# A hybrid attention block in fp32: linear attention's small products set in groups among dense projection products, pooling's vector work ahead of them, output projection by token halves

## The chip, the cores and the metric

The kernel runs on one core of a Trainium2 chip. The metric is the device time of one execution in microseconds, the median of a few runs. TensorE (PE) multiplies matrices; its weight loads (PEld) run beside its products. VectorE (DVE), ScalarE (ACT) and GpSimd (POOL) do the elementwise work, and SyncE's queue (SP) issues nearly all transfers between the DRAM and the on-chip memory. Products land in eight banks of the accumulation memory (PSUM) and are read from there by DVE or ACT.

## The reference

One layer over 1024 tokens of width 1024, batch 1:

```
h = rmsnorm(x, ln1);  z = h @ w_in            # columns split among three mixers
y_pool: trailing means over 2, 4, 8, 16 tokens, minus the input, a 64x64 product per group, a scale
y_gla : linear attention, 4 heads of 64, chunks of 64 tokens:
        q_in = q*exp(b-ref), k_in = k*exp(ref-b), att = tril(q_in k_in^T), o_intra = att v
        kv_n = (k*exp(b_last-b))^T v ;  S_n+1 = dec_n*S_n + kv_n ;  o_inter = (q*exp(b)) S_n
        per-head rmsnorm of o_intra + o_inter, times silu(g)
y_fox : softmax attention with forgetting, 8 heads of 64, causal
x = x + [y_pool, y_gla, y_fox] @ w_o
h = rmsnorm(x, ln2);  x = x + (silu(h@w_gate) * (h@w_up)) @ w_down ;  out = rmsnorm(x, ln_f)
```

## The kernel before, in words

**Tiling.** All data are fp32. A dense product is made of three products of rounded parts: an operand `a` is held as a high part `ah` (rounded, by ACT) and a low part `al = a - ah` (by DVE or POOL), and `gemm` (L133) adds `ah*bh + ah*bl + al*bh` into one PSUM bank, in a fixed order in each bank. A projection of 128 columns of `w_in` (`project`, L243) loads its 128x1024 weights, splits them (`load_w`, `split_w`), and makes two banks (token halves `c` of 512) of 8 x 3 = 24 products each, 48 in all. The small products of linear attention (transposes, `pkv`, `pat`, `po`) and pooling's `py` are plain fp32 and are not split.

**Stages.** (1) The first norm and `gv` (`psg`). (2) `decays` (L262): log gates and their running sums `bc`, on ACT and DVE. (3) `pool_in`: projections `zp0`, `zp1` into `u0`, `u1`. (4) `gla_qk(j)` (L285) for the two head pairs `j`: differences of `bc` on POOL (`d1`, `d2`), their exponentials on ACT, the projections `zgk`, `zgq`, their products with the exponentials, and eight transposes `pk` (L312) into `k2t`. (5) `pool_tile` (L396), tile 1 then tile 0: a chain of shifted sums on DVE (L399, L400, L411, L413 to L415), two products `py` (L420), a scaling on ACT (L421) and a transfer to the DRAM (L422). (6) `gla_state` (L316): 30 products `pkv` of 64x64 per pair and a 15-step scan on DVE (L330). (7) `fox_values(0)` (L426): `psv`, 8 token blocks of 24 products of 256 columns. (8) `gla_out(j)` (L339): the projection `zgg` with silu, and for both halves `c`: 8 products `pat` (L353), a masked copy (L355), for each of 8 (block, head) pairs one product with `attb` (L364) and then two 64x64 products with the state (L368) into `po`, the norm, four transposes `pot` (L384). (9) `fox_qk` and `fox_attend` for four head pairs `p`, each projection among the attention of the pair before. (10) The output projection `pxa` (first four 128-row blocks of the mixed activations) and `pxb` (the last four), 24 products per 128-token block `tb`, 8 blocks each; after each `pxb` block the second norm `norm2` with its transposes into `raw`. (11) The feed-forward products by a seven-product scheme: left operands `left(i)` (L660), weights `right(fi)`, products `m` (L710) and `d` (L916). Products 3 and 5 read only the first token half.

**What sets the order.** The program is traced in the order of the code and a scheduler then orders each engine's instructions by a simulated timeline: program order is the priority, and what is not ready in that simulation, by its inputs or by its buffer, is passed over. On the chip each engine runs its list in order. Buffers are slots of 128x1024 fp32. Rings hand them out strictly in program order: `p` (6 slots, most vector tiles), `pp` (3), `wr` (2, raw weights) and `w` (4, the high and low parts of two weight tiles). A tile may be written only when the tile that had its slot before is read for the last time, by transfers too. PSUM has `s` (3 banks), `pt` (2), `o` (1) and `gm` (2, all dense projections).

Ring `p` before, from the decays on: la0, la1, lft, ones, Fc, d2_0, gk0, gq0, d2_1, gk1, gq1, ps2_1, ps4_1, ps8_1, ps16_1, pd1, py1, ps2_0, ps4_0, pd0, py0, sg0, gy0, ... (each on the slot of the tile six places ahead of it). Ring `w`: zp0, zp1, zgk0, zgq0, zgk1, zgq1, the two halves of wfv0, zgg0, zgg1, zq0, zk0, ... (each on the slots of the one two places ahead). In the output projection `mr4` and `mix4`, the first buffers that `pxb` needs, have the slots of `wo3h` and `wo3l`, which the last `pxa` product reads.

Of the kernel before, what the change touches and what calls it, by code (L numbers as in the profile page):

```python
# [18 lines left out]
P = 128  # L19
# [12 lines left out]
def tile_hybrid_block(ctx: ExitStack, tc, x, w_fv, w_gv, w_zt, w_o, w_gu, w_down, ln, w_pool, w_a3, chans, b_f, consts, out):  # L32
# [107 lines left out]


# [101 lines left out]
    def project(ct, name):  # L243
        hi, lo = load_w(w_zt[:, ct, :], name, eng=POOL)
        for c in range(2):
            ps = PS("gm", f"{name}p{c}")
            gemm(ps, [((hi[:, k * P:(k + 1) * P], lo[:, k * P:(k + 1) * P]), chunk(hT, k, c)) for k in range(NK)])
            yield slice(c * 512, c * 512 + 512), ps
# [11 lines left out]
    decs, bcs = [], []  # L260
# [24 lines left out]
    def gla_qk(j):  # L285
        bc = bcs[j]
        b3 = e3(bc)
        dc = cst.tile([P, 16], F32, name=f"dec{j}")
        decs.append(dc)
        ACT.activation(dc, b3[:, :, 63], AF.Exp, scale=1.0 / 16)  # L290
        d1, d2, eq = G(f"d1_{j}"), R(f"d2_{j}"), G(f"eq{j}")
        POOL.tensor_tensor(out=e3(d1), in0=b3, in1=b3[:, :, 31:32].broadcast_to([P, 16, 64]), op=ALU.subtract)
        POOL.tensor_tensor(out=e3(d2), in0=b3[:, :, 63:64].broadcast_to([P, 16, 64]), in1=b3, op=ALU.subtract)
        ACT.activation(eq, d1, AF.Exp, scale=1.0 / 16)
        ACT.activation(d1, d1, AF.Exp, scale=-1.0 / 16)
        ACT.activation(d2, d2, AF.Exp, scale=1.0 / 16)
        ACT.activation(bc, bc, AF.Exp, scale=1.0 / 16)
        k_, q_ = R(f"gk{j}"), R(f"gq{j}")
        for csl, ps in project(8 + 2 * j, f"zgk{j}"):
            ACT.activation(k_[:, csl], ps, AF.Copy)  # L300
        DVE.tensor_tensor(out=d2, in0=k_, in1=d2, op=ALU.mult)
        DVE.tensor_tensor(out=d1, in0=k_, in1=d1, op=ALU.mult)
        for csl, ps in project(9 + 2 * j, f"zgq{j}"):
            ACT.activation(q_[:, csl], ps, AF.Copy, scale=0.125)
        DVE.tensor_tensor(out=eq, in0=q_, in1=eq, op=ALU.mult)
        POOL.tensor_tensor(out=bc, in0=q_, in1=bc, op=ALU.mult)
        kt = G(f"k2t{j}")
        for h in range(2):
            pt = PS("pt", f"pk{j}_{h}")
            for i in range(4):  # L310
                tb = 4 * h + i
                PE.transpose(pt[:, i * P:(i + 1) * P], d2[:, tb * P:(tb + 1) * P], ident)  # L312
            ACT.activation(kt[:, h * 512:(h + 1) * 512], pt, AF.Copy)
        return eq, d1, bc, kt

    def gla_state(j, kt):  # L316

        St = G(f"St{j}")
        POOL.memset(St[:, 0:64], 0.0)
        ps = [PS("s", f"pkv{j}_{q}") for q in range(2)]  # L320
        for n in range(15):
            tb, r = n // 2, slice(64 * (n % 2), 64 * (n % 2) + 64)
            o = ps[n % 2][:, (n // 2) * 64:(n // 2) * 64 + 64]
            for a in range(2):
                PE.matmul(o[64 * a:64 * a + 64], kt[r, tb * P + 64 * a:tb * P + 64 * a + 64],
                          gv[tb // 4][r, (tb % 4) * 256 + (2 * j + a) * 64:(tb % 4) * 256 + (2 * j + a + 1) * 64],
                          start=True, stop=True)
        for n in range(15):
            o = ps[n % 2][:, (n // 2) * 64:(n // 2) * 64 + 64]
            DVE.scalar_tensor_tensor(out=St[:, (n + 1) * 64:(n + 2) * 64], in0=St[:, n * 64:(n + 1) * 64],  # L330
                                     scalar=decs[j][:, n:n + 1], in1=o, op0=ALU.mult, op1=ALU.add)
        free(f"k2t{j}")
        return St

# [4 lines left out]
    def gla_out(j, qi, ki, qe, St):  # L339
        sg = R(f"sg{j}")  # L340
        for csl, ps in project(12 + j, f"zgg{j}"):
            ACT.activation(sg[:, csl], ps, AF.Silu)
        y = R(f"gy{j}")
        for c in range(2):
            pat = [PS("pt", f"pat{j}_{c}_{a}") for a in range(2)]
            po = [PS("s", f"po{j}_{c}_{a}") for a in range(2)]
            ab = attb[c]
            for i in range(4):
                tb = 4 * c + i
                tsl = slice(tb * P, (tb + 1) * P)  # L350
                for a in range(2):
                    r = slice(64 * a, 64 * a + 64)
                    PE.matmul(pat[a][:, i * P:(i + 1) * P], ki[r, tsl], qi[r, tsl], start=True, stop=True)  # L353
            for a in range(2):
                DVE.copy_predicated(ab[:, a * 512:(a + 1) * 512].rearrange("p (m t) -> p m t", t=P),  # L355
                                    gmask.rearrange("p (o t) -> p o t", o=1).broadcast_to([P, 4, P]),
                                    pat[a].rearrange("p (m t) -> p m t", t=P))
            for i in range(4):
                tb = 4 * c + i
                for a in range(2):  # L360
                    r = slice(64 * a, 64 * a + 64)
# [647 lines left out]
```

## Time and profile before

| | |
|---|---|
| median of 3 runs (lowest to highest) | 1199.56 us (1198.48 to 1200.44) |
| the profiled execution | 1203.56 us |
| its span, first to last instruction | 1201.8 us |
| mean granted TensorE clock | 0.979 of full speed |
| PE busy in the span | 97% |
| DVE / ACT / POOL busy | 67% / 44% / 33% |

The profile is one execution. The span is what the views cover; the profiled execution is 1.8 us longer than its span and 4.0 us (0.33%) above the median of the runs. A matmul's recorded duration is its pipelined time; what a stream of them costs is read from the distance of their starts.

### The profile page before, as it was taken

To read this page: it belongs to the slowest core of one execution; us is meant where nothing else is said; L and a number is where in the kernel's file an instruction comes from. 1 tells how busy PE (TensorE), PEld (TensorE's weight loads), DVE (VectorE), ACT (ScalarE), POOL (GpSimd) and SP (SyncE) were. 2 spreads that over 40 slices of the span, in tenths; PEclk is the share of its full clock that TensorE was granted. 3 is DMA by queue.
4 is the path that set the end of the run, shared out by engine and by line. 5 is a ranking of instruction groups with operands and counts; after the bars stand their busy time and mean duration, and the time that the engine had idled before them with its cause. 6 is when DMAs were issued, how large, how long until landed. Compare 5 with 4: busy or idle time off the path is not lost.

```text
span 1201.8 us, 15933 instructions
## 1 busy us (share of the span) xinstructions
PE 1159.9 (97%) x5928; PEld 974.8 (81%) x5928; DVE 810.2 (67%) x1328; ACT 530.9 (44%) x965; POOL 390.9 (33%) x285
## 2 busy tenths in 40 slices
PE   6999999999999989899999999999999999999995
PEld 6878788889988778777888888888888888888874
DVE  7567612278748676468998768676776685766674
ACT  6362121257656745346444334443343344334353
POOL 2163122243333823331022220122202270660873
PEclk9999889899999999899999999999999999999998
DMA  6121111111122522221153331323224588333223
GB/s 244 35 71 53 54 35 53 36 55 47 47 62 77 169 91 97 79 105 53 53 155 112 111 120 65 131 93 118 95 90 148 214 322 288 109 96 118 63 97 140
DMA packets 53565, 126.34 MB, mean 105 GB/s; under 512 B 4792, under 2 KB 10344, under 8 KB 53488
## 3 DMA queue, kind: packets, MB, share of 16 engines
q1 hardware_dynamic: 53056, 123.75, 30.7%
q0 software_dynamic: 432, 1.57, 0.4%
q8 instruction: 46, 0.75, 0.3%
q14 instruction: 31, 0.25, 0.1%
HBM read 93.03 MB, written 32.28 MB: 104 GB/s over the span
## 4 chain that ended last, share of the span: by engine, by line
PE 84%; DVE 5%; DMA 3%; issue 3%; POOL 3%; ACT 2%; POOLq 0%; SPq 0%; ACTq 0%; DVEq 0%
PE m L710 35%; PE d L916 16%; PE pxa L138 4%; PE psv L138 3%; PE o L524 3%; PE pt L510 2%; PE s L484 1%; PE zq0p L138 1%; PE zgg0p L138 1%; PE s L485 1%; DMA mr<-mixd 1%; PE psg L138 1%; PE po L364 1%; PE zq3p L138 1%; PE zgg1p L138 1%
## 5 line engine op out<-in xcount | busy, mean ns | idle before, releaser
L710 PE MATMUL m<-hA_0h,wr 128*128 128x512 f32 x616 | 214.3, 390 | 0.6 <-ACT hr L641 0.5
L710 PE MATMUL m<-hA_1h,wr 128*128 128x512 f32 x616 | 214.6, 389 | 0.0
L710 PEld LDWEIGHTS m<-hA_0h,wr 128*128 128x128 f32 x616 | 115.6, 188 | 24.9 <-ACT hr L641 1.1
L710 PEld LDWEIGHTS m<-hA_1h,wr 128*128 128x128 f32 x616 | 115.7, 188 | 23.9
L916 PE MATMUL d<-hw,ha 128*128 128x512 f32 x308 | 120.0, 392 | 5.3 <-ACT hw L815 5.3
L710 PE MATMUL m<-hA_0l,wr 128*128 128x512 f32 x308 | 119.9, 389 | 1.7 <-DVE hA_0l L671 1.7
L916 PE MATMUL d<-lw,ha 128*128 128x512 f32 x308 | 120.4, 391 | 0.8 <-DVE lw L816 0.8
L710 PE MATMUL m<-hA_1l,wr 128*128 128x512 f32 x308 | 119.8, 389 | 0.0
L762 POOL TENSOR_TENSOR cg<-cu,cu 128x512 f32<-128x512 f32 x11 | 19.2, 1742 | 308.7 <-DVE cu L739 308.7
L916 PE MATMUL d<-hw,la 128*128 128x512 f32 x308 | 118.8, 391 | 0.0
L694 ACT ACTIVATE wr<-ws 128x512 fp32r<-128x512 f32 x110 | 69.5, 631 | 109.2 <-DVE ws L693 54.9
L695 DVE TENSOR_TENSOR wr<-ws,wr 128x512 fp32r<-128x512 f32 x110 | 75.9, 696 | 26.0 <-ACT wr L694 26.0
L816 DVE TENSOR_TENSOR la<-ra,ha 128x1024 fp32r<-128x1024 f32 (+1 forms) x42 | 58.2, 1392 | 29.0 <-ACT ha L815 21.5
L808 POOL TENSOR_TENSOR rw<-wd,wd 128x512 f32<-128x512 f32 x33 | 56.4, 1737 | 51.3 <-PE d L916 46.6
L916 PEld LDWEIGHTS d<-hw,ha 128*128 128x128 f32 x308 | 58.1, 189 | 17.8 <-ACT hw L815 5.7
L710 PEld LDWEIGHTS m<-hA_0l,wr 128*128 128x128 f32 x308 | 57.8, 188 | 14.2 <-DVE hA_0l L671 2.2
L916 PEld LDWEIGHTS d<-lw,ha 128*128 128x128 f32 x308 | 58.3, 189 | 13.3 <-DVE lw L816 1.2
L815 ACT ACTIVATE ha<-ra 128x1024 fp32r<-128x1024 f32 (+1 forms) x42 | 41.2, 987 | 61.6 <-DMA ra<-cd 56.0
L916 PEld LDWEIGHTS d<-hw,la 128*128 128x128 f32 x308 | 58.1, 189 | 12.1
L710 PEld LDWEIGHTS m<-hA_1l,wr 128*128 128x128 f32 x308 | 57.8, 188 | 12.1
L499 POOL TENSOR_TENSOR pb<-pb,rl 128x128 f32<-128x128 f32 (+3 forms) x32 | 38.1, 1196 | 83.4 <-DVE rl L496 66.5
L816 DVE TENSOR_TENSOR lw<-rw,hw 128x1024 fp32r<-128x1024 f32 (+1 forms) x30 | 45.7, 1535 | 27.3 <-ACT hw L815 27.2
(391 smaller groups left out, 2764.1 us busy)
## 6 DMA issues: line engine op xcount, KB each, us to landing
ra<-cd SPq DMA_DIRECT2D x35, 512.0 KB, 3.7
wu<-in_w_gu_dram SPq DMA_DIRECT2D x22, 512.0 KB, 4.3
wg<-in_w_gu_dram SPq DMA_DIRECT2D x22, 512.0 KB, 3.7
wd<-in_w_down_dram SPq DMA_DIRECT2D x22, 512.0 KB, 6.5
cd<-cg SPq DMA_DIRECT2D x11, 512.0 KB, 4.6
cd<-cs SPq DMA_DIRECT2D x11, 512.0 KB, 6.2
cd<-cu SPq DMA_DIRECT2D x11, 512.0 KB, 7.5
fb<-Fd SPq DMA_DIRECT2D x8, 512.0 KB, 4.5
```

What stands on the lines that cost most here:

```text
L138: PE.matmul(ps, a, b, start=(n == 0), stop=(n == last))
L499: POOL.tensor_tensor(out=pb[:, 0:W], in0=pb[:, 0:W], in1=rl[:, 0:1].broadcast_to([P, W]), op=ALU.mult)
L510: PE.transpose(pt[:, o0:o0 + P], Pb[i][:, (2 * n + b) * P:(2 * n + b + 1) * P], ident)
L524: PE.matmul(*args, start=(kb == 0 and n_ == 0), stop=(last and n_ == 1))
L694: ACT.activation(hi, src, AF.Copy)
L695: e2.tensor_tensor(out=lo, in0=src, in1=f(hi), op=ALU.subtract)
L710: PE.matmul(ps, a, b, start=(n == 0), stop=(n == 11))
L762: POOL.tensor_tensor(out=t_[:, 0:512], in0=a11, in1=a12, op=ALU.add)
L808: POOL.tensor_tensor(out=raw_[:, j * 512:j * 512 + 512], in0=wd[h0, j0 + j][:, e0, :], in1=wd[h1, j0 + j][:, e1, :], op=op)
L815: ACT.activation(hi[:, sl], src, AF.Copy)
L816: DVE.tensor_tensor(out=lo[:, sl], in0=src, in1=f(hi[:, sl]), op=ALU.subtract)
L916: PE.matmul(banks[t], a[:, o], b[:, ns], start=(j0 + j == 0 and m == 0), stop=(j0 + j == NF // 2 - 1 and m == 2))
```

## The change

The small products become lists of functions that a projection calls between its dense products (`woven`, `smalls`). `Gla` takes the place of `gla_qk`, `gla_state` and `gla_out`. Within a part of `outputs`, four products with `attb` come first and then eight with the state. `pool_tile` is traced ahead of all of linear attention. The weights of the six projections of linear attention are split on DVE and no longer on POOL. The last head pair's attention runs m = 1, 0, 3, 2 in place of 3, 1, 2, 0; the output projection's halves `g` are tokens 0 to 511 and 512 to 1023; products 3 and 5 of the feed-forward get their left operands, and `start(0)` its weights, after four of the eight `pxb` blocks.

Ring `p` after: la0, la1, lft, ones, Fc, ps2_1, ps4_1, ps8_1, ps16_1, pd1, py1, ps2_0, ps4_0, pd0, py0, d2_0, gk0, gq0, sg0, gy0, d2_1, gk1, gq1, sg1, gy1, ... Ring `w` after: zp0, zp1, zgk0, zgq0, zgg0, zgk1, zgq1, zgg1, the two halves of wfv0, zq0, zk0, ...

```
+    def woven(ps, terms, smalls=()):
+        done = 0
+        for i, ((ah, al), (bh, bl)) in enumerate(terms):
+            for n, (a, b) in enumerate(((ah, bh), (ah, bl), (al, bh))):
+                PE.matmul(ps, a, b, start=(i == 0 and n == 0), stop=(i == len(terms) - 1 and n == 2))
+            while done < len(smalls) and (done + 1) * len(terms) <= (i + 1) * len(smalls):
+                smalls[done]()
+                done += 1
...
-    def project(ct, name):
-        hi, lo = load_w(w_zt[:, ct, :], name, eng=POOL)
+    def project(ct, name, smalls=((), ()), eng=None):
+        hi, lo = load_w(w_zt[:, ct, :], name, eng=eng or POOL)
         for c in range(2):
             ps = PS("gm", f"{name}p{c}")
-            gemm(ps, [...])
+            woven(ps, [...], smalls[c])
...
+    class Gla:
+        def keys(self, smalls=((), ())):
+            j, k_ = self.j, R(f"gk{self.j}")
+            for csl, ps in project(8 + 2 * j, f"zgk{j}", smalls, eng=DVE):
+                ACT.activation(k_[:, csl], ps, AF.Copy)
+            DVE.tensor_tensor(out=self.d2, in0=k_, in1=self.d2, op=ALU.mult)
+            DVE.tensor_tensor(out=self.d1, in0=k_, in1=self.d1, op=ALU.mult)
...
+        def outputs(self, c):
+            def part(i2):
...
+                both = [(i, a) for i in (2 * i2, 2 * i2 + 1) for a in range(2)]
+                for i, a in both:
+                    h = 2 * j + a
+                    PE.matmul(po[a][:, i * 64:i * 64 + 64], attb[c][:, (4 * a + i) * P:(4 * a + i + 1) * P],
+                              gv[c][:, i * 256 + h * 64:i * 256 + (h + 1) * 64], start=(i == 0), stop=False)
+                for i, a in both:
+                    r = slice(64 * a, 64 * a + 64)
+                    for q in range(2):
+                        n = 2 * (4 * c + i) + q
+                        PE.matmul(po[a][64 * q:64 * q + 64, i * 64:i * 64 + 64], self.bc[r, n * 64:(n + 1) * 64],
+                                  self.St[r, n * 64:(n + 1) * 64], start=False, stop=(i == 3))
+                if i2:
+                    normed()
...
     us = [pool_in(j) for j in range(2)]
-    g0 = gla_qk(0)
-    g1 = gla_qk(1)
     pool_tile(1, us[1])
     pool_tile(0, us[0])
     free("misc")
-    st0 = gla_state(0, g0[3])
-    st1 = gla_state(1, g1[3])
-    V = fox_values(0)
-    gla_out(0, g0[0], g0[1], g0[2], st0)
-    gla_out(1, g1[0], g1[1], g1[2], st1)
+    A = Gla(0)
+    A.keys()
+    A.queries(((), A.turn_keys()))
+    A.gates((A.state(), A.within(0)))
+    B = Gla(1)
+    B.keys((A.within(1) + A.outputs(0), A.outputs(1) + A.turned(0)))
+    B.queries((A.turned(1), B.turn_keys()))
+    B.gates((B.state(), B.within(0)))
+    o_ = [B.outputs(0), B.outputs(1)]
+    V = fox_values(0, (B.within(1), o_[0][:1], o_[0][1:], o_[1][:1], o_[1][1:] + B.turned(0), B.turned(1), (), ()))
     ops = fox_qk(0)
...
-        for a, m in ([...] if p < 3 else [(a, m) for m in (3, 1, 2, 0) for a in range(2)]):
+        for a, m in ([...] if p < 3 else [(a, m) for m in (1, 0, 3, 2) for a in range(2)]):
...
-            SP.dma_start(src, mixd[k].rearrange("p (c g t) -> p c g t", c=2, g=2)[:, :, g])
+            SP.dma_start(src, mixd[k, :, g * 512:(g + 1) * 512])
...
-        for tb in (2 * g, 2 * g + 1, 2 * g + 4, 2 * g + 5):
+        for tb in range(4 * g, 4 * g + 4):
...
-    mixes = [load_mix(4, g) for g in (1, 0)][::-1]
-    for tb in (2, 3, 6, 7, 0, 1, 4, 5):
-        g = (tb // 2) % 2
-        out_proj(tb, xs[tb], mixes[g], ws, "pxb")
...
-    first = [start(fi) for fi in range(2)]
+    mixes = [load_mix(4, 0), None]
+    first = []
+    for tb in range(NT):
+        if tb == 2:
+            mixes[1] = load_mix(4, 1)
+        if tb == 4:
+            free(*[f"mix{k}_0" for k in range(4, 8)])
+            for i in (3, 5):
+                left(i, *lefts[i])
+            first.append(start(0))
+        out_proj(tb, xs[tb], mixes[tb // 4], ws, "pxb")
+        SP.dma_start(x3d[tb], xs[tb])
+        norm2(tb, xs[tb])
+        free(f"xa{tb}")
...
+    first.append(start(1))
     for i in (3, 5, 4, 1, 2, 7, 6):
-        left(i, *lefts[i])
+        if i not in (3, 5):
+            left(i, *lefts[i])
```

## Rows read from the trace of the kernel before

**Rows 1.** The page's first two parts: PE's busy time, its share of the span and its instructions; the TensorE clock granted in 40 slices of the span, in tenths (9 is 90% or more).

```profile
PE 1159.9 (97%) x5928; PEld 974.8 (81%) x5928; DVE 810.2 (67%) x1328; ACT 530.9 (44%) x965; POOL 390.9 (33%) x285
...
PEclk9999889899999999899999999999999999999998
```

**Rows 2.** Busy time by stretch. Columns: the stretch in us and its length, then busy us (and instructions) of PE, PEld, DVE, ACT, POOL, the mean granted clock (1.00 is 2.4 GHz, 0.50 is 1.2 GHz), the share of the DMA engines' time, GB/s.

```profile
128.00:136.00 8.00, 7.65 (x22) 4.52 (x22) 3.96 (x11) 1.82 (x4) 0.00 (x0) 0.57 0.04 16
136.00:162.00 26.00, 26.00 (x297) 23.60 (x296) 11.40 (x43) 5.27 (x15) 0.00 (x0) 1.00 0.10 37
...
165.00:177.00 12.00, 12.00 (x45) 8.62 (x46) 1.61 (x4) 2.05 (x3) 3.73 (x2) 0.57 0.30 87
...
206.00:218.00 12.00, 12.00 (x53) 9.44 (x54) 2.22 (x5) 0.77 (x2) 1.64 (x1) 0.57 0.01 1
...
400.00:440.00 40.00, 33.10 (x174) 27.53 (x173) 29.84 (x63) 26.55 (x50) 27.58 (x21) 0.91 0.44 143
...
491.00:504.00 13.00, 9.12 (x42) 7.60 (x41) 4.26 (x8) 4.90 (x11) 6.13 (x7) 0.74 0.22 82
...
553.00:562.00 9.00, 6.50 (x33) 4.58 (x32) 7.09 (x9) 6.15 (x14) 0.55 (x1) 1.00 0.15 60
```

**Rows 3.** PE's timeline: start, us, engine, line, what is written from what, count (one plain fp32 product has two records). First the outputs' alternation at the full clock, then the same at the lower clock, then dense products at the lower clock and at the full clock.

```profile
163.61 0.43 PE L364 MATMUL po<-gv,attb 128*128 128x64 f32 x2
...
164.24 0.43 PE L364 MATMUL po<-gv,attb 128*128 128x64 f32 x2
...
167.69 0.69 PE L364 MATMUL po<-gv,attb 128*128 128x64 f32 x2
...
168.72 0.69 PE L364 MATMUL po<-gv,attb 128*128 128x64 f32 x2
...
173.88 1.05 PE L138 MATMUL zgg0p<-hT,zgg0h 128*128 128x512 f32 x2
...
175.16 1.05 PE L138 MATMUL zgg0p<-hT,zgg0h 128*128 128x512 f32 x2
...
180.64 0.62 PE L138 MATMUL zgg0p<-hT,zgg0h 128*128 128x512 f32 x2
...
181.32 0.62 PE L138 MATMUL zgg0p<-hT,zgg0h 128*128 128x512 f32 x2
```

**Rows 4.** PE's timeline again, in order: the first query product, the transposes of the second pair's keys (one record each) and the product behind them, the wait in front of `pat` (in brackets: idle time and what ended it), the last product `py`, the stream of `pkv` and what follows it.

```profile
83.49 0.62 PE L138 MATMUL zgq0p<-hT,zgq0h 128*128 128x512 f32 x2
...
117.84 1.03 PE L312 MATMUL pk<-ident,d 128*128 128x128 f32 x8
118.63 0.36 PE L138 MATMUL psv<-wfv_0h,hT 128*128 128x256 f32 x1
...
128.35 2.05 PE L353 MATMUL pat<-eq,d 64*128 64x128 f32 x10 [1.89 <-DVE ps L414]
...
137.60 1.13 PE L420 MATMUL py<-pd,misc 128*128 128x512 f32 x2
138.66 2.43 PE L325 MATMUL pkv<-gv,k2t 64*64 64x64 f32 x92
141.02 0.38 PE L138 MATMUL psv<-wfv_0h,hT 128*128 128x256 f32 x1
```

**Rows 5.** DVE's timeline: the two running sums of the decays, then steps of pooling's chain.

```profile
70.73 2.29 DVE L277 TENSOR_TENSOR_SCAN bc<-reset,la 128x1024 f32<-128x1024 f32 x1
...
74.17 3.91 DVE L277 TENSOR_TENSOR_SCAN bc<-reset,la 128x1024 f32<-128x1024 f32 x1
...
96.25 0.15 DVE L399 COPY ps<-u 128x1 f32<-128x1 f32 x1 [2.45 <-PE pk L312]
96.32 1.21 DVE L400 TENSOR_TENSOR ps<-u 128x1023 f32<-128x1023 f32 x1
...
108.16 2.90 DVE L411 COPY ps<-ps 64x1024 f32<-64x1024 f32 x1
...
126.38 1.28 DVE L413 SCALAR_TENSOR_TENSOR pd<-ps,misc,u 128x1024 f32<-128x1024 f32 x1
```

**Rows 6.** POOL's timeline: a difference of the decays, a split of weights.

```profile
75.89 3.88 POOL L293 TENSOR_TENSOR d<-bc 128x1024 f32<-128x1024 f32 x1
...
108.12 2.39 POOL L113 TENSOR_TENSOR wfv_0l<-wfv_0r,wfv_0h 128x1024 fp32r<-128x1024 f32 x1 [5.00 <-ACT wfv_0h L112]
```

**Rows 7.** ACT's timeline: the last part of `u1`, a scaled copy of `py`, the high part of zgg0's weights.

```profile
74.14 0.58 ACT L393 ACTIVATE u<-zp1p 128x512 f32<-128x512 f32 x1
...
132.49 0.69 ACT L421 ACTIVATE py<-py,ch 128x512 f32<-128x512 f32 x1 [2.91 <-issue]
...
161.22 1.06 ACT L112 ACTIVATE zgg0h<-zgg0r 128x1024 fp32r<-128x1024 f32 x1 [1.60 <-PE psv L138]
```

**Rows 8.** The instructions on the tile `py`: the time from issue to landing of its two transfers to the DRAM. And, of the instructions of L113, a split of weights on DVE (durations in ns, min/median/max).

```profile
DMA to landing us min/median/max: 2.6/3.7/4.7
...
L113 DVE TENSOR_TENSOR wgv1l<-wgv1r,wgv1h x1: 1028/1028/1028, 14.9 to 14.9; 128x840 fp32r<-128x840 f32 x1
```

**Rows 9.** PE's timeline from the end of `pxa` to the first feed-forward products, with the waits in front of them.

```profile
491.54 0.39 PE L138 MATMUL pxa<-wo3h,mix 128*128 128x512 f32 x1
...
498.51 0.79 PE L138 MATMUL pxb<-wo4h,mix 128*128 128x512 f32 x1 [2.84 <-ACT mix L562]
...
555.95 0.50 PE L710 MATMUL m<-hA_0l,wr 128*128 128x512 f32 x1 [1.72 <-DVE hA_0l L671]
```

More of the change, by code (lines that the diff above doesn't have):

```diff
@@ L259, in tile_hybrid_block @@
     DVE.memset(e3(reset)[:, :, 0:1], 0.0)
[L260 removed]
+    bcs = []
     def decays():
@@ L283, in decays @@
         free("fx")
[L285 to L333, printed above, removed]
@@ L531, in fox_item @@
         else:
-            hi, lo = (last_mix[m % 2][rows, h, (m // 2) * 256:(m // 2 + 1) * 256] for h in range(2))
+            hi, lo = (last_mix[m // 2][rows, h, (m % 2) * 256:(m % 2 + 1) * 256] for h in range(2))
             ACT.activation(hi, oy[rows], AF.Copy)
@@ L541, in fox_attend @@
             fbs.append(fb)
-        for a, m in ([(a, m) for a in range(2) for m in range(4)] if p < 3 else [(a, m) for m in (3, 1, 2, 0) for a in range(2)]):
+        for a, m in ([(a, m) for a in range(2) for m in range(4)] if p < 3 else [(a, m) for m in (1, 0, 3, 2) for a in range(2)]):
             fox_item(p, a, m, ops, fbs[a], V)
@@ L643, in norm2 @@
         free(f"n2sq{tb}")
-    mixes = [load_mix(4, g) for g in (1, 0)][::-1]
-    for tb in (2, 3, 6, 7, 0, 1, 4, 5):
-        g = (tb // 2) % 2
-        out_proj(tb, xs[tb], mixes[g], ws, "pxb")
-        SP.dma_start(x3d[tb], xs[tb])
-        norm2(tb, xs[tb])
-        free(f"xa{tb}")
-        if tb in (7, 5):
-            free(*[f"mix{k}_{g}" for k in range(4, 8)])
-    free("wo6h", "wo6l", "wo7h", "wo7l", "ln2b")
-    idle.extend(rings.pop("wr") + rings.pop("w"))
-    hA = {}
-    def left(i, in0, in1=None, op=None):
-        hA[i] = []
-        for kp in range(2):
-            hi, lo = (G(f"hA{i}_{kp}{h}", F32R).rearrange("p (k t) -> p k t", k=2) for h in "hl")
-            src = raw[in0][kp]
-            if in1 is not None:
-                t_ = G(f"hs{i}{kp}").rearrange("p (k t) -> p k t", k=2)
-                DVE.tensor_tensor(out=t_, in0=src, in1=raw[in1][kp], op=op)
-                src = t_
-                free(f"hs{i}{kp}")
-            ACT.activation(hi, src, AF.Copy)
-            DVE.tensor_tensor(out=lo, in0=src, in1=f(hi), op=ALU.subtract)
-            hA[i].append((hi, lo))
     cd = dpool.tile([7, NF // 2, P, 512], F32, name="cd")
@@ L823, in prep, with left @@
             ready.append(ops)
+    hA = {}
+    def left(i, in0, in1=None, op=None):
+        hA[i] = []
+        for kp in range(2):
+            hi, lo = (G(f"hA{i}_{kp}{h}", F32R).rearrange("p (k t) -> p k t", k=2) for h in "hl")
+            src = raw[in0][kp]
+            if in1 is not None:
+                t_ = G(f"hs{i}{kp}").rearrange("p (k t) -> p k t", k=2)
+                DVE.tensor_tensor(out=t_, in0=src, in1=raw[in1][kp], op=op)
+                src = t_
+                free(f"hs{i}{kp}")
+            ACT.activation(hi, src, AF.Copy)
+            DVE.tensor_tensor(out=lo, in0=src, in1=f(hi), op=ALU.subtract)
+            hA[i].append((hi, lo))
     seen = []
@@ L841, in tile_hybrid_block @@
              6: (2, 0, ALU.subtract)}
-    first = [start(fi) for fi in range(2)]
+    mixes = [load_mix(4, 0), None]
[12 more added lines that the diff above has]
+        free(f"xa{tb}")
+    free("wo6h", "wo6l", "wo7h", "wo7l", "ln2b", *[f"mix{k}_1" for k in range(4, 8)])
+    idle.extend(rings.pop("wr") + rings.pop("w"))
+    first.append(start(1))
     for i in (3, 5, 4, 1, 2, 7, 6):
-        left(i, *lefts[i])
+        if i not in (3, 5):
+            left(i, *lefts[i])
         if i == 7:
@@ L887, in final @@
             SP.dma_start(out[tb * P:(tb + 1) * P, ns], x2[:, ns])
-        free(f"c{tb}")
     def add_down(i, t, bank):
```

161 lines of the change are left out of this document (107 added, 54 removed).

## The prediction

> **What bounds the kernel now.** The page first: PE is busy 97% of the span and its clock is full in nearly all of it [rows 1]. The reader is to see that only the stretches in which PE waits, is clocked down, or spends more than its products need can give time back. A table by stage finds them: three stretches around linear attention with a mean clock of 0.57, and three around the output projection with idle PE [rows 2]. PE's timeline then gives the price of each kind of product at both clocks [rows 3, 4]; the vector engines' timelines and the transfers of `py` give the chain that pooling will put in front [rows 5 to 8]. The sum is made against the profiled execution (1203.56 us) and then taken off the median, 4.0 us lower (1199.56).
>
> **Linear attention, the clock.** A mean of 0.57 between the levels 1.0 (2.4 GHz) and 0.5 (1.2 GHz) says that 86% of a stretch ran at the lower one: 6.9, 10.3 and 10.3 us, together 27.5 [rows 2]. Before each fall PE had a wait (1.89 us in front of `pat`) or a run of small products [rows 3, 4]. What a low microsecond loses: three dense products start 1.28 us apart at the low level and 0.68 at the full one (47% lost); an outputs group takes 1.03 against 0.63 (39%) [rows 3]. At 43%, 27.5 us lose 11.8. From 136 to 162 us small products stood among `psv` products and the clock stayed at 1.00 [rows 2], which is what the change makes of all of them. I take the whole 11.8 (bounds 6 and 13) and the 1.89 of idle time.
>
> **The outputs in groups.** Before, each of 32 (block, head) pairs takes one product with `attb` and two with the state, 0.63 us a pair [rows 3]: 20.2 in all. After, a part is four of the first kind and then eight of the second, and there are 8 parts. No row has two of the first kind in a row; a transpose, which loads 128 columns of weights too, takes 0.10 us a record (8 in 0.79), and a first-kind product is two records: 0.2, bounds 0.11 and 0.36 (the distance inside the alternation, weights and switch included). The 64x64 products cost 2.36 us for 92 records in a row, two records each, so 0.05 [rows 4]. A pair alone is thus 0.3 of the 0.63, and two switches of shape take the rest, some 0.15 each. A part is 4 x 0.2 + 8 x 0.05 + 0.3 = 1.5, eight are 12; 8.2 come off (bounds 4 and 11). Against it stand the groups themselves: some 20 groups of 64-row products among dense ones switch twice each, 6 us, of which the 17 runs that PE's timeline shows before paid 5. So 1 us more.
>
> The Trainium skill has a rule on just this, and by itself it speaks against setting small groups among dense products: a change of the tiling mode drains TensorE ("TensorEngine Tiling (Array Packing)", section "Key Properties"). The trace agrees, at the 0.15 us a switch worked out above; the rule gives no price, and counting only the 20 new groups by it, without the 17 old ones, the time would be 5 us higher.
>
> **Pooling first: a new wait.** Ring `p` hands its slots out in program order. With pooling ahead, gk0 follows py1, d2_0 follows pd1. So `zgk0p` can be read out of its two `gm` banks only when py1 has left for the DRAM, and the first query product needs such a bank. No other dense product can step in: ring `w` and `gm` are in order too. The chain: the decays' last running sum ended at 78.1 in the trace; it took 3.91 us beside POOL's difference where the other took 2.29 [rows 5, 6], and zgk0's split leaves POOL and costs DVE some 1.25 us (1.03 for 840 columns, scaled) [rows 8]. Together I put its end at 76 (75 to 78); `u1` is ready at 74.7 [rows 7], earlier. Then tile 1: four steps of 0.15 + 1.21, the copy L411 (2.90 beside a POOL split; bound below 0.2, by the short copies), 1.28, two small ones of 0.2: 9.9 [rows 5, 6]. One more split on DVE, zgq0's, 1.25. So pd1 at 87 (85 to 90). Two `py` products 2.1 (1.06 each) [rows 4], the scaled copy 0.69 [rows 7], the transfer 3.7 (2.6 to 4.7) [rows 8], gk0's copy 0.58 as u1's [rows 7]: 7.1. The first query product comes at 94 (91 to 98), where it was 83.49 [rows 4]. PE has py1's 2.1 us in between, moved from later, and perhaps half of py0's: 7.5 us idle (4 to 11). After the 1.89 us wait the clock was low for 6.9 us, so the same again at 43%, part of it under `py`: 2.5. Cost: 10 (6 to 14). ACT's list has gk0's copy waiting at its head, and behind it the exponentials of d2_0, which nobody needs before the query product's second half; DVE's and POOL's work goes on.
>
> One price in this chain is a page's. The Trainium skill has fp32 copies inside SBUF run at two elements a cycle ("VectorE: DVE Perf Modes", section "Mode 2×_2P"), an estimate of 0.53 us for L411's 1024 columns at 0.96 GHz; the row shows 2.90, with POOL active, and no run here shows it alone. By the page the wait would be 2.4 us shorter and the time 1189.3.
>
> **Hand-overs.** Before, `psv` held all of ring `w` and zgg0's weights came after it; small products filled that gap. After, zq0 comes there with nothing small left. ACT's high part (1.06) [rows 7] and POOL's low part (2.39) [rows 6] start when half of the last block remains: some 2 us idle, and a low stretch behind it: 3.5 (0 to 6). The other five splits moved to DVE have a whole projection (48 x 0.227 = 10.9 us) as cover, and DVE is half busy or less in the stretches shown around linear attention [rows 2]; if that cover failed, each would cost its 1.25. Small products that come due in PE's list before their vector work is done: 1 (0 to 5), by the one such wait of 1.89. Transfers of `y` and of the weights are the same in number; SP has DMA share to spare [rows 2].
>
> **Output projection.** Between 553 and 562 us PE is idle 2.5 us [rows 2], 1.72 of it for the left operand of a first product [rows 9]; after, products 3 and 5 of the first column block have their operands four blocks earlier, so this wait goes; late next is `raw` of the second half for product 4, covered by less work than before. I take 2.5 off and 1 back. From 491 to 504 PE loses 3.9 us idle and runs at 0.74, since the first `pxb` waits for a transfer into slots that the last `pxa` product reads (491.54 to 498.51) [rows 2, 9]; both slots are the same after, so this stays. From 400 to 440 6.9 us are idle [rows 2]; light items first bring less PE work and less POOL work, the heavy ones come behind: 0 (3 either way). The contiguous transfers of the mix move the same bytes. Sum -1.5 (-5 to +4).
>
> **Sum.** -11.8 - 1.9 - 8.2 + 1 + 10 + 3.5 + 1 - 1.5 = -7.9: 1195.7 for a profiled execution, **1191.7** for the median. The likeliest case's own range is 1183 to 1200: the bounds of six terms, which won't all fall on one side.
>
> **Rivals.** (a) The new wait is small: pooling's chain runs undisturbed, py1 is out before the keys' banks are full. For it: DVE's steps are slow only beside POOL. Against it: even with every low bound the query product comes at 91. All 10 us of the wait fall out: 1181.7. Chance 0.18. (b) The new wait decides, and the kernel is slower. Place: `zgk0p`'s banks behind py1's transfer. Break-even is a first query product at 102. If tile 0's steps (7.2 us by the same rows) or linear attention's are set between tile 1's on DVE, it comes at 105, with a longer low stretch of 3 more: +14 - 7.9, 1205.7. For it: in the trace other work stands between pooling's steps, which spread from 96 to 128 us [rows 5]. Against it: they waited for slots there, which are free now. Chance 0.15. (c) The weaving comes about only in part: small products not ready in the scheduler's simulation are passed over and collect as before. For it: it already set them among `psv` products, and two of the three falls came from those left over. Half of the clock's gain stays out: 1197.6. Chance 0.17. The forecast has 0.5.
>
> **Numbers.** Some 0.2% (2.4 us) is what a measurement of this kernel can tell from no change. Below 1197.2 lie most of the forecast, all of (a) and not quite half of (c): 0.39 + 0.18 + 0.08 = 0.65. Within 0.2% lie 0.07 of the forecast and 0.07 of (c): 0.14. Above lie (b) whole and what is left of the others: 0.21. The range 1179 to 1205 leaves out a tenth at each end.
>
> **What would show it.** Right: the clock at 1.00 from the first gate projection to the end of `psv`; `po` at some 1.5 us a part; an idle PE of 4 to 11 us ahead of `zgq0p`, ended by ACT's gk0; no wait of `m` for `hA`; `pxb` still behind the mix's transfer. Wrong: stretches near 0.57 that remain in linear attention, `zgq0p` before 88 or after 102, or more than 4 us of change from `pxa` on.

## The result, and the profile after

The changed kernel takes **1188.05 us** (median of 4 runs, 1187.57 to 1189.15), the kernel before 1199.02 in the same comparison: 11.0 us less, ratio 0.9902 (95% interval 0.9881 to 0.9924). The forecast was 7.9 us less. The sign and the range held, but about half of the gain came from a line of the diff that was not in the sum at all.

First the page's lines that answer to [rows 1].

```profile
PE 1137.7 (96%) x5928; PEld 958.9 (81%) x5928; DVE 813.9 (69%) x1334; ACT 533.0 (45%) x965; POOL 372.0 (31%) x279
...
PEclk9998999999999999998999999999999999999998
```

The slices at 8 in linear attention (the fifth, sixth and eighth) are gone; there is one now at the fourth, and the one of the output projection went from the seventeenth to the nineteenth, where it ends. The table by stage, with the columns of [rows 2], shows it closer.

```profile
88.00:96.00 8.00, 3.87 (x5) 1.70 (x6) 5.64 (x10) 0.82 (x2) 0.09 (x1) 0.57 0.22 66
...
102.00:106.00 4.00, 4.00 (x12) 3.13 (x11) 1.86 (x2) 0.36 (x1) 2.44 (x1) 0.57 0.13 53
106.00:136.00 30.00, 30.00 (x212) 23.92 (x210) 11.81 (x22) 8.30 (x11) 2.88 (x1) 1.00 0.12 36
136.00:162.00 26.00, 26.00 (x188) 21.78 (x187) 9.16 (x16) 6.91 (x12) 4.27 (x3) 1.00 0.07 21
165.00:177.00 12.00, 12.00 (x94) 9.64 (x93) 5.13 (x16) 2.14 (x3) 3.21 (x2) 1.00 0.10 37
206.00:218.00 12.00, 10.60 (x54) 8.77 (x53) 2.02 (x5) 3.63 (x6) 4.73 (x2) 1.00 0.38 123
400.00:440.00 40.00, 34.70 (x194) 29.32 (x195) 33.40 (x74) 25.48 (x54) 23.28 (x20) 0.96 0.41 129
...
549.00:557.00 8.00, 6.09 (x19) 4.96 (x20) 5.58 (x6) 6.01 (x13) 0.44 (x1) 0.57 0.00 0
```

From 106 us to the end of `psv` the clock stays at 1.00 (2.4 GHz). The longest falls that are left stand around a new wait of pooling (88 to 106) and, new too, at the end of the output projection (549 to 557). PE's timeline has the wait, and the grouped outputs that answer to [rows 3, 4] (x8 and x16 records are a whole part, x4 and x8 a half).

```profile
83.44 0.39 PE L146 MATMUL zgk0p<-hT,zgk0l 128*128 128x512 f32 x1
92.13 5.42 PE L476 MATMUL py<-pd,misc 128*128 128x512 f32 x8 [8.30 <-DVE pd L471]
100.95 0.73 PE L146 MATMUL zgq0p<-hT,zgq0h 128*128 128x512 f32 x2 [3.41 <-ACT gk L320]
...
135.25 1.10 PE L404 MATMUL po<-gv,attb 128*128 128x64 f32 x8
136.28 0.46 PE L410 MATMUL po<-St,bc 64*64 64x64 f32 x16
136.67 0.50 PE L146 MATMUL zgk1p<-hT,zgk1h 128*128 128x512 f32 x1
...
140.74 0.55 PE L404 MATMUL po<-gv,attb 128*128 128x64 f32 x4
141.22 0.45 PE L410 MATMUL po<-St,bc 64*64 64x64 f32 x8
141.60 0.74 PE L146 MATMUL zgk1p<-hT,zgk1h 128*128 128x512 f32 x2
```

A part takes 1.42 us from start to the next dense product; where the scheduler cut it in two, a half takes 0.86.

Last, the end of the kernel, which none of the rows ahead of the prediction shows. The diff has one more line, in `final`, which stands neither in the diff above nor in the prediction:

```
             SP.dma_start(out[tb * P:(tb + 1) * P, ns], x2[:, ns])
-        free(f"c{tb}")
```

In the kernel before, the slots of the finished output tiles c0 to c3 went back into the list of free slots, which is served in order of return, and four pieces of the down projection's last item (`ha`, `la` and `hw`, halves of its operands, and the weight sum `rw`) got them. So the last weight sum on POOL waited until an output had left for the DRAM, and PE's last products waited for its split. Timelines of POOL and PE, kernel before:

```profile
1181.45 1.26 POOL L808 TENSOR_TENSOR rw<-wd,wd 128x512 f32<-128x512 f32 x1 [3.45 <-DMA out_dram<-c]
...
1183.43 1.22 PE L916 MATMUL d<-hw,ha 128*128 128x512 f32 x2 [5.26 <-ACT hw L815]
```

Busy time over 20 us there, up to some 4 us before PE's last product: before, and after. PE has 60 products in the first and 90 in the second.

```profile
1170.00:1190.00 20.00, 14.74 (x60) 11.72 (x59) 11.44 (x17) 7.92 (x18) 10.12 (x10) 0.91 0.28 105
```

```profile
1154.00:1174.00 20.00, 20.00 (x90) 16.55 (x89) 16.66 (x21) 11.63 (x27) 11.91 (x11) 1.00 0.28 103
```

PE was idle 5.3 us there, and the mean clock of the stretch was 0.91; now there is no idle time and the clock is at 1.00.

### The profile page after: what moved, and what is told of

Its sections match the earlier page's. It is cut to its first block, busy times and chain, and to the rows that moved or that the text cites. A ratio compares the mean times of both kernels' runs of the same rounds, so it can differ in the third digit from the quotient of the medians.

```text
span 1187.2 us, 15923 instructions
## 1 busy us (share of the span) xinstructions
PE 1137.7 (96%) x5928; PEld 958.9 (81%) x5928; DVE 813.9 (69%) x1334; ACT 533.0 (45%) x965; POOL 372.0 (31%) x279
## 4 chain that ended last, share of the span: by engine, by line
PE 81%; DVE 4%; issue 2%; DMA 2%; ACT 2%; POOL 1%; POOLq 0%; SPq 0%; ACTq 0%; DVEq 0%
PE m L740 35%; PE d L981 15%; PE psv L146 4%; PE pxa L138 3%; PE o L580 2%; PE pt L566 2%; PE pxb L138 2%; PE s L540 1%; PE s L541 1%; PE zgq0p L146 1%; PE zgk1p L146 1%; PE zgg0p L146 1%; PE zgg1p L146 1%; PE zq3p L146 1%; PE zk3p L146 1%
## 5 line engine op out<-in xcount | busy, mean ns | idle before, releaser
L740 PE MATMUL m<-hA_0h,wr 128*128 128x512 f32 x616 | 215.2, 391 | 0.0
L725 DVE TENSOR_TENSOR wr<-ws,wr 128x512 fp32r<-128x512 f32 x110 | 78.5, 720 | 17.7 <-ACT wr L724 17.7
L838 POOL TENSOR_TENSOR rw<-wd,wd 128x512 f32<-128x512 f32 x33 | 60.8, 1869 | 46.9 <-PE d L981 46.8
L981 PEld LDWEIGHTS d<-lw,ha 128*128 128x128 f32 x308 | 57.8, 188 | 12.1
L846 DVE TENSOR_TENSOR lw<-rw,hw 128x1024 fp32r<-128x1024 f32 (+1 forms) x30 | 48.9, 1639 | 21.7 <-ACT hw L845 21.5
```

The costliest lines, as they stand in the source:

```text
L725: e2.tensor_tensor(out=lo, in0=src, in1=f(hi), op=ALU.subtract)
L740: PE.matmul(ps, a, b, start=(n == 0), stop=(n == 11))
L838: POOL.tensor_tensor(out=raw_[:, j * 512:j * 512 + 512], in0=wd[h0, j0 + j][:, e0, :], in1=wd[h1, j0 + j][:, e1, :], op=op)
L846: DVE.tensor_tensor(out=lo[:, sl], in0=src, in1=f(hi[:, sl]), op=ALU.subtract)
L981: PE.matmul(banks[t], a[:, o], b[:, ns], start=(j0 + j == 0 and m == 0), stop=(j0 + j == NF // 2 - 1 and m == 2))
```

## The experiments

Each was compared with the kernel before on one chip. The table has the ratio with its interval, and what was read from PE's timeline of each profiled execution: the start of the first query product and of the last `zk0` (linear attention is over), then the distances to the last gate product `m` and to PE's end, and how long the clock was at the lower level between 72 us and that `zk0`. A profiled execution lies up to 4.7 us from its kernel's median, so small differences in these columns tell nothing. Differences between two changed kernels are given by their medians; by their ratios they come out up to some 2 us otherwise.

| kernel | ratio (95%) | zgq0 | zk0 | zk0 to m | m to end | low |
|---|---|---|---|---|---|---|
| before | 1 | 83.5 | 238.7 | 738.1 | 218.0 | 27.3 |
| after | 0.9902 (0.9881 to 0.9924) | 101.0 | 231.0 | 736.8 | 209.9 | 10.2 |
| e_gla_only | 0.9939 (0.9922 to 0.9957) | 101.2 | 231.1 | 732.3 | 217.7 | 13.7 |
| e_out_only | 0.9952 (0.9940 to 0.9965) | 83.6 | 237.1 | 733.4 | 211.1 | 23.9 |
| e_one_line | 0.9942 (0.9920 to 0.9963) | 83.3 | 235.5 | 738.7 | 211.0 | 20.5 |
| e_freed | 0.9959 (0.9942 to 0.9976) | 101.3 | 231.3 | 737.0 | 217.7 | 10.2 |
| e_no_wait | 0.9871 (0.9853 to 0.9888) | 90.4 | 223.9 | 736.0 | 209.9 | 6.8 |
| e_keys_free | 0.9810 (0.9780 to 0.9839) | 83.7 | 219.8 | 735.1 | 209.9 | 3.4 |
| e_alternate | 1.0031 (1.0014 to 1.0047) | 101.0 | 240.8 | 735.7 | 211.1 | 20.5 |
| e_behind | 0.9872 (0.9844 to 0.9900) | 100.6 | 226.3 | 735.1 | 209.9 | 10.2 |
| e_groups_only | 0.9927 (0.9903 to 0.9951) | 83.5 | 228.9 | 738.0 | 217.9 | 17.1 |
| e_two_edits | 0.9865 (0.9834 to 0.9897) | 82.5 | 226.3 | 732.4 | 211.0 | 13.7 |
| e_best | 0.9791 (0.9763 to 0.9820) | 83.2 | 217.5 | 731.3 | 209.8 | 0.0 |
| e_best2 | 0.9767 (0.9736 to 0.9798) | 84.1 | 215.2 | 737.3 | 210.2 | 0.0 |

**The two halves of the change.** Linear attention alone, and the output projection's part alone (that last line with it).

> The changed kernel with the output projection as before (items of the last pair in the old order, mix in interleaved quarters, token blocks in the old order, the first gate products behind the last block). Theory (the gain is in linear attention alone): zk0 ended 7.7 us earlier by the trace and the output projection gave 1 to 2 us net: 1188 to 1191. Rival A (the output projection's new order gave as much as linear attention: the last gate product ended 9.1 us earlier and the profiled spans differ by 14.6): 1193 to 1196. Rival B (it costs, since idle PE between pxb and m grew by 3 us of waiting on the norm's product and the clock fell there): 1184 to 1187.

> The kernel before with the output projection's part of the change alone. Theory: 1 to 2 us less than before, 1197 to 1198, and with the other half alone the two add up to the whole gain of 11 within 1.5 us. Rival A: 3 to 6 us less, 1193 to 1196. Rival B: 1 to 4 us more, 1200 to 1203, as the first pxb still waits for its transfer and the norm's product waits for its square.

Measured 1190.66 and 1192.57 us: 7.0 and 5.1 less, together 12.1, which is the whole gain of 11.0 within the 1.5 us expected. The first is the theory's. The second has the size of its rival A, but not for A's reason: what moved is the way from the last `m` to PE's end, shorter by 6.9 us.

**The last line.** The kernel before without it (a blank line in its place), and the changed kernel with it put back.

```
-        free(f"c{tb}")
+
```

> The kernel before with the change's last line alone: the slots of the final tiles c are no longer handed back after their output (the diff takes that line out, and the prediction does not mention it). Theory: in the kernel before, the last pieces of the down projection sit in slots of c0 to c3, so the last weight sum on POOL waits for an output transfer, and PE waits 5.3 and 0.8 us for it, with a low clock behind. Without the line these pieces follow weights and splits that were read long before: 6 to 8.5 us less, ratio 0.993 to 0.995, and from the last gate product to PE's end 210 us in place of 218. Rival (the output projection's new order is what changed the end, by other slots): no change within 2 us and a wait of d for hw that stays above 4 us.

> The changed kernel with the one line put back that hands the final tiles' slots on. Theory: the wait at the end of the down projection comes back (5 to 6 us and a low clock behind it), 6 to 8 us more than the changed kernel: 1194 to 1196, ratio 0.996 to 0.998; what is left, 2 to 5 us less than before, is what the rest of the change gives after its new wait. Rival (with other slots the wait falls on other tiles and is short): 0 to 3 us more, ratio 0.990 to 0.993.

Measured 1191.63 and 1193.68: the one line takes 6.7 us off the kernel before, and putting it back costs the changed kernel 5.6. The first theory held; of the second the wait came back and the size is just short of its 6 to 8 us (by the ratios it is 6.8). In the table, the four kernels that hand the slots back have 217.7 to 218.0 us from the last `m` to PE's end, the others 209.8 to 211.1. PE's timeline of e_freed has the wait again, with the rest of the change in place:

```profile
1174.68 1.22 PE L982 MATMUL d<-hw,ha 128*128 128x512 f32 x2 [5.11 <-ACT hw L845]
```

With this line apart, three pairs tell the output projection's order: e_freed against e_gla_only, e_out_only against e_one_line, e_keys_free against e_best. In each the new order is the slower one, by 3.0, 0.9 and 2.7 us, where each of these times has an interval of 1.5 to 3.5 us to either side: none is clear of noise. From `zk0` to the last `m` the profiled executions scatter by 7 us and tell no difference (means of 735.6 and 735.4). So no gain of it can be seen; it may have cost up to 3.

**The new wait.** First pooling's `pd` and `py` were moved out of ring `p`.

```
-        d = R(f"pd{j}")
+        d = G(f"pd{j}")
...
-        y = R(f"py{j}")
+        y = G(f"py{j}")
```

> The changed kernel with pooling's last two tiles, pd and py, taken from the list of free slots instead of ring p, so that gk0 follows ps4_1 (long read) and no longer py1. Theory (the new wait is a cost by itself): in the changed kernel's trace PE is idle 8.3 us for pd and 3.4 us for gk ahead of the first query product, and clocked down for 6.8 and 3.5 us around it. With the dependence gone the first query product comes at 83 to 86 instead of 100.95, and 12 to 16 us fall out: 1172 to 1176. Rival (the wait only shows how late the vector engines are: the difference, pooling and the splits stand in DVE's list in that order, whoever waits): the wait comes back in front of pk, pkv or pat, as a wait for d2, eq or kt, and at most 4 us fall out: 1184 to 1188.

Measured 1182.37, between the two and for neither's reason. Taking tiles out of a ring moves every later one: `gk0` now followed `ps4_1`, which pooling's third step reads. ACT's timeline has its copy still late, released by DVE at 89.7 (that step ended then; the view names the small DVE instruction behind it), and PE waited 6.8 us for it.

```profile
89.75 0.60 ACT L320 ACTIVATE gk<-zgk0p 128x512 f32<-128x512 f32 x1 [5.53 <-DVE pd L471]
```

So the keys' own tiles were moved instead.

```
-            self.d1, self.d2, self.eq = G(f"d1_{j}"), R(f"d2_{j}"), G(f"eq{j}")
+            self.d1, self.d2, self.eq = G(f"d1_{j}"), (R if j else G)(f"d2_{j}"), G(f"eq{j}")
...
-            j, k_ = self.j, R(f"gk{self.j}")
+            j, k_ = self.j, (G if self.j == 0 else R)(f"gk{self.j}")
...                                   # gq0 in the same way
     A.queries(((), A.turn_keys()))
+    free("d2_0", "gk0", "gq0")
```

> The changed kernel with the first keys' three tiles (d2, gk, gq of block 0) taken from free slots instead of ring p, so that they follow nothing of pooling's. The run with pd and py moved still waited 6.8 us for gk, which then followed ps4_1, read by pooling's third step. Theory (slots alone hold the first query product): it comes at 83 to 84.5, no idle time ahead of it, no fall of the clock there; against the changed kernel 14 to 18 us less, 1170 to 1174. Rival (vector engines: d2 and eq of linear attention are late behind pooling's steps on DVE, and a wait of 3 us or more appears in front of pk, pkv or pat, with a fall of the clock behind): 1176 to 1183.

Measured 1177.51, 10.5 us less than the changed kernel. PE's timeline has no wait left in front of the query product, and a short one in front of `pk`:

```profile
83.52 0.39 PE L146 MATMUL zgk0p<-hT,zgk0l 128*128 128x512 f32 x1
83.75 0.62 PE L146 MATMUL zgq0p<-hT,zgq0h 128*128 128x512 f32 x2
...
94.70 0.66 PE L345 MATMUL pk<-ident,d 128*128 128x128 f32 x4 [1.96 <-DVE d L321]
```

The first query product comes when the theory has it (83.75), but the time is the rival's (1176 to 1183): a wait for DVE appears in front of `pk`, of 2.0 us and not the rival's 3, and a fall of the clock of 3.4 us stands behind it. The new wait cost the changed kernel 10.5 to 11.2 us net of this (medians; start of the last `zk0`).

**Groups.** The outputs alternating again in the changed kernel (the state's loop put inside the first one), and grouping alone in the kernel before.

```
-                for i, a in both:
                     r = slice(64 * a, 64 * a + 64)
```

> The changed kernel with the outputs of linear attention alternating again: each product with attb is followed by its two products with the state. Theory (what groups save is the switching of the product's shape): a part of four and eight took 1.3 to 1.4 us where it stood whole in the changed kernel's trace, and 1.7 to 1.8 where it stood in two halves; alternating it should take 4 x 0.63 = 2.5, so 8 parts cost 6 to 9 us more: 1194 to 1197. Rival (the alternation was dear only because the clock was low or it stood in long runs without dense products between; set among dense products it costs little): 0 to 2 us more, 1188 to 1190, or, if the runs of alternating products let the clock fall again as they did before, 1200 and above.

> The kernel before with one thing of the change: in linear attention's outputs each part does its four products with attb first and then its eight with the state. Nothing is woven, pooling stays where it was. Theory (grouping is what mattered: alternation brought back 7 and 3 us of lower clock and 9.8 us up to the end of zk0, while small products set behind their projections cost nothing): the falls of 10 and 10 us behind the two runs of outputs shrink by half or more, and 6 to 14 us are saved, ratio 0.988 to 0.995. Rival (a fall needs only a long run of small products, grouped or not; before's runs stay long): the falls stay, 3 to 6 us are saved through fewer changes of shape, ratio 0.995 to 0.998.

Measured 1201.36 and 1189.17. Alternation costs the changed kernel 13.3 us, the second branch of the rival: the price of the switches, and 10.2 us more at the lower clock. This kernel has everything else of the change, the last line too, and is no faster than the kernel before (1.0031): without the groups the rest, its new wait included, gains nothing. PE's timeline of e_alternate, and its table by stage:

```profile
133.65 0.43 PE L404 MATMUL po<-gv,attb 128*128 128x64 f32 x2
...
136.16 0.50 PE L146 MATMUL zgk1p<-hT,zgk1h 128*128 128x512 f32 x1
...
137.36 0.69 PE L404 MATMUL po<-gv,attb 128*128 128x64 f32 x2
```

```profile
136.00:146.00 10.00, 10.00 (x54) 7.83 (x55) 1.61 (x4) 1.36 (x3) 1.65 (x1) 0.66 0.01 2
```

A whole part takes 2.51 us there, 1.42 in groups: 1.09 for six changes of product shape, 0.18 each if they are all of it. Grouping alone takes 8.5 us off the kernel before (some 3 to either side), the size that its theory has, and ends linear attention earlier (228.9) than the whole change does (231.0). The falls shrank less than the theory's half: from 10.2 and 10.2 us behind the outputs to one of 13.7. It begins at 193.4, behind 4.1 us of small products, and goes on through 8.5 us more of them, as PE's timeline and the table by stage of e_groups_only show:

```profile
189.23 1.16 PE L353 MATMUL pat<-eq,d 64*128 64x128 f32 x8
...
193.34 1.15 PE L138 MATMUL zq0p<-hT,zq0h 128*128 128x512 f32 x2
194.28 0.95 PE L362 MATMUL po<-gv,attb 128*128 128x64 f32 x4
```

```profile
190.00:208.00 18.00, 18.00 (x108) 15.07 (x107) 3.69 (x7) 1.86 (x5) 3.99 (x2) 0.62 0.10 30
```

**The place of the groups.** `woven` issues a half's small products behind its dense ones.

```
-            while done < len(smalls) and (done + 1) * len(terms) <= (i + 1) * len(smalls):
-                smalls[done]()
-                done += 1
+        for small in smalls:
+            small()
```

> The changed kernel with each set of small products behind the 24 triples of its projection half instead of between them (the same sets, in the same order, and the scheduler may still set them among what follows). Theory (it is their place among dense products that keeps the clock): falls of the clock come back in linear attention, together 6 to 20 us at the lower level, and 3 to 10 us are added: 1191 to 1198. Rival A (the groups are enough, their place is not what matters; the scheduler sets them among the next projection as it did with psv before): within 2 us, 1186 to 1190, the clock full from 106 us on. Rival B (fewer switches than in the woven order): 1 to 3 us less.

Measured 1184.23, 3.8 us less than the changed kernel (the intervals overlap), 4.7 by the last `zk0`: rival B, a little above its size. The theory fell. The table by stage has no fall behind the pooling wait, though the small products no longer stand inside a projection's half:

```profile
106.00:136.00 30.00, 30.00 (x246) 24.56 (x244) 12.30 (x22) 8.34 (x12) 2.87 (x1) 1.00 0.12 36
136.00:200.00 64.00, 64.00 (x559) 56.74 (x552) 24.62 (x54) 12.81 (x31) 14.69 (x7) 1.00 0.10 34
```

Counted on PE's timeline from 72 to 245 us, the product's kind (the tile written and the shapes, all dense products taken as one) changes 103 times in the kernel before, 71 in the changed one, 54 here, 69 in e_groups_only.

**Put together.** Two small edits on the kernel before; linear attention's half with free keys and kept slots; the same with the groups behind.

> The kernel before with two small edits and nothing else: the outputs' products in groups, and the final tiles' slots not handed back. Theory (the two act in different stages and add): 8.5 and 6.9 us less, together some 15: 1181 to 1184, ratio 0.985 to 0.989, so less than the whole change takes. Rival (part of the one is lost by the other, as an earlier end of linear attention shifts which waits decide later): 10 to 12 us less, ratio 0.990 to 0.992, no better than the whole change.

> Linear attention's half of the change, the output projection as before, the first keys' tiles in free slots and the final tiles' slots not handed back. Theory: the output projection's new order gave nothing of its own (from the first pxb to the last gate product 480.4 us in the changed kernel's trace, 476.3 with the old order), so this is the fastest of all: 2 to 5 us less than the run with the new order and the same keys, 1166 to 1172. Rival (the new order is worth the 1.5 us that the prediction gave it, or more): 0 to 3 us slower than that run.

> The fastest run so far (linear attention's half, first keys in free slots, output projection as before, final slots kept) with each set of small products behind its projection half. Theory (fewer changes of shape: 54 in place of 71 in linear attention where this was done alone, zk0's end 4.7 us earlier): 2 to 5 us less than the same kernel woven, ratio 0.975 to 0.978. Rival (there the gain came from the run of py and pk that followed another wait; without that wait nothing is left, or the first pk waits longer): within 1.5 us of the woven kernel, 0.978 to 0.981.

Measured 1182.70, 1174.81 and 1169.63. The two small edits add up to 16.3 us, against 11.0 for the whole change, though the two intervals just overlap. e_best has the same two edits and all the rest of linear attention's half, with the new wait taken out; it is some 8 us faster than they are, clear of noise. So weaving, pooling first and the moved splits are worth something together once the wait is gone; none of the three was run by itself. e_best is 2.7 us under e_keys_free, the sign that was expected, within the noise, and both lie some 3 us above their expected times. e_best2 is the fastest, 28 us (2.3%) less than the kernel before; its lead of 5.2 us over e_best (0.0024 by ratio, 2.9 us) has the expected sign, but the two intervals overlap.

## Why the prediction was right, and where it was not

**The sum came within 3.1 us, some of it by luck: two errors partly offset.** Linear attention: forecast -6.4, measured -7.0 by e_gla_only. The output projection: forecast -1.5, measured 1 to 3 the other way, within the noise. The last line of the diff: not in the sum, measured -5.6 to -6.7. The prediction's own test for being wrong, more than 4 us of change from `pxa` on, was met: that stretch is 9.9 us shorter (403.9 to 1194.7 before, 396.8 to 1177.7 after), 8.1 of it behind the last `m`. The step that failed is the first one, on what bounds the kernel: the views by stage were read around the edits, and the wait of 5.3 us at the end, which PE's list of waits shows, was left out with the line that makes it.

**The clock** (-11.8, and -1.9 for the wait before `pat`). The falls of [rows 2] are gone and PE no longer waits for `pat`. The size was read from one execution: the same code shows 27.3, 23.9 and 20.5 us at the lower level in three (before, e_out_only, e_one_line), which the forecast's 43% would price at 8.8 to 11.7 us. The cause given, small products standing among dense ones, is not what the runs single out: e_behind keeps the clock with the small products behind their dense ones, and e_alternate loses it with the weaving in place. What they show is the grouping: with it undone and nothing else, 10.2 us of falls come back (one execution of each). Why grouping keeps the clock stays open. In e_alternate the first fall begins at 137.1, in the second of two runs of small products (3.6 and 3.7 us, 0.6 of dense ones between), the second at 205.3, behind another of 3.7 us. In e_behind two grouped runs of 3.9 and 3.7 us, with 5.6 of dense products between, keep the clock; in e_groups_only it falls behind a grouped one of 4.1. And one stretch, `pat`, `py` and `pkv` behind the wait for `pat`, has a fall of 3.4 us in e_groups_only and none in e_two_edits, with the same code there. So the kind of the products, the length of a run and the dense work between runs are not told apart.

**The groups** (-8.2) were right as a price: 1.32 and 1.42 us a whole part and 1.72 one cut in two, against 1.5 forecast, and 0.18 us a change of shape against 0.15. The Trainium skill's rule that a change of tiling mode drains TensorE ("TensorEngine Tiling (Array Packing)", section "Key Properties") is what e_alternate, e_groups_only and e_behind agree with: fewer changes, less time, at the 0.18 us above. **The extra switches** (+1) point the right way but were too few: PE's timeline has 25 runs of small products, not 20, against 17 before, and e_behind, with 17, is 3.8 us faster (the intervals overlap).

**The new wait** (+10; rival b). Place and price were right: 10.5 measured. Its parts were not, so the price is luck. DVE, POOL and ACT, changed kernel, from the timelines that answer to [rows 5 to 7]:

```profile
73.83 3.91 DVE L287 TENSOR_TENSOR_SCAN bc<-reset,la 128x1024 f32<-128x1024 f32 x1
77.67 1.19 DVE L113 TENSOR_TENSOR zgq0l<-zgq0r,zgq0h 128x1024 fp32r<-128x1024 f32 x1
78.78 2.95 DVE L456 TENSOR_TENSOR ps<-u 128x1023 f32<-128x1023 f32 x1
...
84.37 1.22 DVE L456 TENSOR_TENSOR ps<-u 128x1023 f32<-128x1023 f32 x1
...
86.89 1.22 DVE L456 TENSOR_TENSOR ps<-ps 64x1022 f32<-64x1022 f32 x1
88.03 1.30 DVE L467 COPY ps<-ps 64x1024 f32<-64x1024 f32 x2
89.36 1.28 DVE L469 SCALAR_TENSOR_TENSOR pd<-ps,misc,u 128x1024 f32<-128x1024 f32 x1
90.57 1.22 DVE L113 TENSOR_TENSOR zgg0l<-zgg0r,zgg0h 128x1024 fp32r<-128x1024 f32 x1
...
91.90 0.17 DVE L471 TENSOR_TENSOR pd<-ps,u 128x16 f32<-128x16 f32 x1
```

```profile
77.82 2.83 POOL L310 TENSOR_TENSOR d<-bc 128x1024 f32<-128x1024 f32 x1 [2.23 <-DVE bc L287]
```

```profile
96.73 0.69 ACT L477 ACTIVATE py<-py,ch 128x512 f32<-128x512 f32 x1 [0.17 <-PE py L476]
97.84 1.06 ACT L311 ACTIVATE d<-d 128x1024 f32<-128x1024 f32 x1 [0.42 <-POOL d L309]
98.80 1.04 ACT L314 ACTIVATE bc<-bc 128x1024 f32<-128x1024 f32 x1
99.75 0.67 ACT L477 ACTIVATE py<-py,ch 128x512 f32<-128x512 f32 x1
100.32 1.07 ACT L320 ACTIVATE gk<-zgk0p 128x512 f32<-128x512 f32 x2
```

`pd1` ended at 92.1, not 87. The last running sum ended at 77.7, not 76, since it took 3.91 us again. Two of tile 0's steps, its copy and zgg0's split stand between tile 1's steps (4.3 us), which is rival (b)'s own place, and the first step, beside POOL, took 1.7 us more than forecast; the copy took 2.2 us less. Then `py` began at the lower clock, and ACT had two exponentials and a copy ahead of `gk0`'s. The transfer, too, was shorter than taken, 2.6 us for both against 3.7 [rows 8]. The query product came at 100.95, past the 91 to 98 of the forecast and 1 us short of its break-even of 102. By the forecast's price, 10 us at 94 and one more for each later us, that would have cost 17 and left almost no gain. It cost 10.5 to 11.2: of the 17.4 us by which the product moved, 5.4 are `py`, which is work moved and not lost, and the kernel without the wait pays 2.0 us of another wait and a fall of 3.4 us that the changed one doesn't have. The break-even was too early, then. **Rival (a)**, the small wait, did not come; e_keys_free shows what it would have given. **Rival (c)** did not come either: the small products stand inside their projections, as the timeline of `zgk1` above has them.

**Hand-overs** (+3.5): `zq0` waited 1.4 us and no fall followed (206 to 218 in the table by stage), so 2 us too much. **In-order waits** (+1): none of size. **The output projection**: `m` waits 0.4 us for its left operand, where it was 1.72 [rows 9], and `pxb` still waits for the mix, 2.5 us; but the norm's transposes, which the text named only as covered "by less work than before", now wait 1.1 and then 3.1 us, and in the second wait the clock falls for 6.8 us (549 to 557). e_out_only shows the same two waits without linear attention's half. PE's waits after `pxa`, changed kernel:

```profile
PE n2pt L698 <- DVE n2sq L693: 3.1, 1, 3.1
PE pxb L138 <- ACT mix L618: 2.5, 1, 2.5
PE n2pt L698 <- ACT hr L700: 1.1, 1, 1.1
...
PE m L740 <- DVE hA_0l L869: 0.4, 1, 0.4
```

## What to carry to other kernels

Cost every line of a diff, a dropped `free` too: who gets that slot next, and what must have left it by then. Where tiles share a ring or a list of slots, moving one moves the waits of all behind it, so follow the list to the next tile before a wait is called gone. Before weaving small products through large ones, put the small ones of one shape side by side; in this kernel that alone gave 8.5 us where the whole change gave 11.0, and the rest of the change without it, new wait included, gained nothing.

## What the runs showed of the hardware

The copy that the forecast took at 2.90 us, from a row beside a POOL split [rows 5, 6], takes 0.65 us with POOL idle (two in 1.30, changed kernel). That is near the estimate of 0.53 from the Trainium skill ("VectorE: DVE Perf Modes", section "Mode 2×_2P"), and far from 2.90.

A DVE sum of two inputs that takes 1.22 us alone took 2.95 when a POOL difference had begun 0.96 us earlier, and ended 1.08 us after it. The Trainium skill says that a DVE instruction with two SBUF inputs contends with a GpSimd instruction that reads SBUF, for ports that are locked to one of them at a time ("SBUF — State Buffer", section "Who interferes with whom"). The rows agree: what is left after POOL's end is nearly the whole 1.22.
